# A conformer convolution: one channel tile's taps as products of token pairs, the last tile by token blocks, sums and second factor inside the norm's wait

## The chip, the cores and the metric

The kernel runs on one core of a Trainium2 chip. The metric is the device time of one execution in microseconds, given as the median of several runs; the time of before is 931.02 us (three runs, 930.98 to 931.54). Beside the runs there is one profiled execution, whose trace shows every engine: PE is TensorE (matrix products), PEld its weight loads, DVE VectorE, ACT ScalarE, POOL GpSimd, SP the engine that issues most DMAs.

## The reference

A trunk of two layers over 256 tokens of 1024 channels in float32. Each layer is half a SwiGLU FFN, a mixer, half a SwiGLU FFN, each behind an RMS norm and added to the residual stream; a final norm ends it. The mixer of the first layer is the convolution module, that of the second a latent attention. The change is in the convolution module:

```python
CONV_WIDTH = 31
def conv_module(h, w_pw1, w_dw, g_norm, w_pw2):
    u = h @ w_pw1                                  # 1024 -> 2048
    a, b = jnp.split(u, 2, axis=-1)
    u = a * jax.nn.sigmoid(b)
    u = lax.conv_general_dilated(                  # causal, depthwise: 31 taps per channel
        u, w_dw[:, None, :].astype(u.dtype), window_strides=(1,),
        padding=[(CONV_WIDTH - 1, 0)], dimension_numbers=("NWC", "WIO", "NWC"),
        feature_group_count=D_MODEL)
    u = jax.nn.silu(rmsnorm(u, g_norm))            # norm over the 1024 channels
    return u @ w_pw2                               # 1024 -> 1024
...
def reference(x, ...):
    h = x
    for i in range(DEPTH):
        h = h + 0.5 * swiglu_ffn(rmsnorm(h, ffn_norm1[i]), ...)
        m = rmsnorm(h, mix_norm[i])
        h = h + (conv_module(m, ...) if i % 2 == 0 else mla(m, ...))
        h = h + 0.5 * swiglu_ffn(rmsnorm(h, ffn_norm2[i]), ...)
    return rmsnorm(h, final_norm)
```

## The kernel before

**Weights.** All matrices come from memory as blocks of 128x2048 float32 (1 MB) through three raw buffers, in the order of the list `blocks`; a load is issued on SP and waits there until its raw buffer is free. Most blocks are split for TensorE into a high part (ScalarE copies to the reduced type float32r, L162) and a low part (VectorE subtracts, L163), in two pieces each, into five buffer pairs. A product of split factors is three products, low by high, high by high and high by low (`mm3`, and `mm` in the convolution with kinds "l", "h", "x"). The blocks of the convolution's first matrix (`cw1`, one for each of eight tiles of 128 channels) are used whole, from the raw buffer, without a split.

**Order.** The program is written in order and then scheduled; `order(a, b)` puts a behind b on an engine, functions marked `urgent` get priority, and `behind` puts a cast behind the last six urgent instructions of its engine. Each engine runs its own queue in the order that results, and waits at an instruction until its inputs are there.

**The convolution** (`conv_in`). Channels lie on partitions, tokens along the free dimension: eight tiles of 128 channels by 256 tokens. The tokens are two blocks of 128.

- *Projection* (`products`, L640). For each tile a gate and a factor u, each a sum over eight products of plain float32. Tiles 0 and 1 are done by token block, the others for 256 tokens at once, in the order of `CONV_STEPS` (0, 1, 2, 4, 3, 5, 6, 7). ScalarE makes the sigmoid of the gate (L649), VectorE multiplies (L650) into `V`, which has 30 zero columns ahead of the tokens.
- *Taps.* 31 taps for each tile. VectorE does tiles 0, 2, 4 and 5 and 17 taps of tile 7 (`taps_dve`, L684), one instruction a tap, accumulating in two PSUM banks. GpSimd does tiles 1 and 3 and 20 taps of tile 6 (`taps_pool`, L706): ScalarE writes the product of a tap into one of six buffers (L705), GpSimd adds it. TensorE does the remaining 11 taps of tile 6 and 14 of tile 7, for each token block (`taps_pe`, L716), as products with a 128x128 diagonal matrix, which ScalarE builds during the first FFN. Tiles 6 and 7 are the last ones (`CONV_LAST`) and are done by token block; an addition on VectorE (L818) joins their parts.
- *Norm.* ScalarE squares each tile (L728), TensorE sums over the channels by a product with ones of one column (`total`, L734). In `normed` ScalarE takes the mean (L749), GpSimd the power -1/2 (L751), ScalarE puts it on a diagonal (L753), TensorE spreads it over the partitions (`rb`, L761), VectorE scales (z, L768), ScalarE applies silu twice, once into the high part `Zh` (L772), and VectorE subtracts for the low part `Zl` (L774). This is done for each token block; `ends` starts it.
- *Second matrix* (`mm`, L849). For each token block eight steps f, in each of them six products of 512 columns. The first block's products run while the second block's taps are finished; the second block's sums stand behind step 4, its `rb` behind step 6, and the products of step 7 behind that.

The four blocks of the second matrix (`cw2`) are cast to high and low parts; three are loaded ahead of the blocks of `cw1`, the fourth behind them.

Of the kernel before, what the change touches and what calls it, by code (L numbers as in the profile page):

```python
# [29 lines left out]
PAD = TAPS - 1  # L30
H = 8
# [20 lines left out]
CONV_STEPS = ((0, 0), (1, 0), (0, 1), (1, 1), (2, None), (4, None), (3, None), (5, None), (6, None), (7, None))  # L52
CONV_TILES = (0, 1, 2, 4, 3, 5, 6, 7)
CONV_LAST = (7, 6)

CONV_ORDER = (0, 2, 1, 4, 5, 3, 7, 6)
# [23 lines left out]
def trunk(ctx: ExitStack, tc: tile.TileContext, x, xt, pos, invf, gains, gfin, wdw,  # L80
# [28 lines left out]
    for i in range(2):  # L109
        for w13, w2 in ((f1w13, f1w2), (f2w13, f2w2)):  # L110
# [33 lines left out]
    def load(src, pieces=1):  # L144
# [15 lines left out]
        for i in range(pieces):  # L160
            c = slice(i * n // pieces, (i + 1) * n // pieces)
            casts[len(loaded), i] = (nc.scalar.copy(hi[:, c], raw[:, c]),  # L162
                                     nc.vector.tensor_sub(lo[:, c], raw[:, c], hi[:, c].bitcast(F32)))  # L163
# [460 lines left out]
    def conv_in(act, X, make_next):  # L624
# [4 lines left out]
        Y = act.tile([P, KT, S], F32, tag="Y", name="Y")  # L629

        acc = [bank(t, "acc") for t in "CB"]
        for a in acc:
            behind(nc.vector.memset(a, 0.0))

        def products(i, part, t, u, after=None):

            w = loaded[conv_block[i]]
            for k in range(KT):
                c = slice(k * 2 * P + part * P, k * 2 * P + (part + 1) * P)
                mm = nc.tensor.matmul(u[:, t], w[:, c], X.x[:, k, t], start=(k == 0), stop=(k == KT - 1))  # L640
                if after is not None:
                    order(mm, after.ins)
            return mm

        @urgent
        def glu(i, t, gate, u):
            n = t.stop - t.start
            sg = tmp.tile([P, 512], F32, tag="s", name=uid("sg"))
            nc.scalar.activation(sg[:, :n], gate[:, t], AF.Sigmoid)  # L649
            nc.vector.tensor_mul(V[:, i, PAD + t.start:PAD + t.stop], u[:, t], sg[:, :n])  # L650

        every = slice(0, S)
        mm = None
        for n, (i, tb) in enumerate(CONV_STEPS):
# [8 lines left out]
            glu(i, t, gate, u)  # L663

        behind(nc.scalar.activation(small.tile([P, 1], F32, tag="silu", name="silu2"), neghalf, AF.Silu))

# [23 lines left out]
        def taps_pool(k, j0, j1, t):  # L690
# [3 lines left out]
            if k not in odd:  # L694
                odd[k] = act.tile([P, S], F32, tag="odd", name=uid("odd"))
            y = [(part[k] if k in part else Y[:, k, :])[:, t], odd[k][:, t]]
# [12 lines left out]
        def taps_pe(t, done):  # L709

            b = bank("A", "y")
            y = {}
            for i, (k, j0, j1) in enumerate(CONV_PE):
                y[k] = b[:, i * P:(i + 1) * P]
                for j in range(j0, j1):
                    mm = nc.tensor.matmul(y[k], diag[k][:, j - j0, :], V[:, k, j + t.start:j + t.stop],  # L716
                                          start=(j == j0), stop=(j == j1 - 1))
                    done.append(mm)
            return y

# [4 lines left out]
        def square(k, t):  # L725
            if k not in sq:
                sq[k] = act.tile([P, S], F32, tag="sq", name=uid("sq"), bufs=4)
# [18 lines left out]
        def normed(tb, after=()):  # L746
# [7 lines left out]
            if tb == 0:  # L754

                for ins in pool_last[-16:]:
                    order(ins, power.ins)
                order(prods_last[-6], ms_ins.ins)
                order(prods_last[-4], dgs[0].ins)
# [17 lines left out]
            if tb == 0:  # L777

                for ins in dve_last[-5:]:
                    order(ins, zs[1].ins)  # L780
                for ins in prods_last[-7:]:
                    order(ins, zhs[1].ins)

        for items, taps in ((CONV_DVE, taps_dve), (CONV_POOL, taps_pool)):
            for item in items:
                if item[0] in CONV_FIRST:
                    for tb in range(NT):
                        taps(*item, tbs(tb))
                elif item[0] not in CONV_LAST:
                    taps(*item, every)  # L790
# [4 lines left out]
        y, done = {}, {0: [], 1: []}  # L795
        sums = {}
        for tb in range(NT):
            t = tbs(tb)
            for item in CONV_DVE:
                if item[0] in CONV_LAST:  # L800
                    taps_dve(*item, t)
            for item in CONV_POOL:
                if item[0] in CONV_LAST:
                    taps_pool(*item, t)
            if tb == 0:
                for k in CONV_ORDER:
                    if k not in CONV_LAST:
                        for i in range(NT):
                            total(k, i)
            y[tb] = taps_pe(t, done[tb])  # L810
        def ends(tb, after, after_row):
# [4 lines left out]
            def add():  # L816
                for k in CONV_LAST:
                    last = nc.vector.tensor_add(Y[:, k, t], y[tb][k], part[k][:, t] if k in part else Y[:, k, t])  # L818
                    if tb == 1:

                        order(last, zs[3].ins)
                    sq_ins = square(k, t)
                    if tb == 0:

                        for ins in dve_last[3 - CONV_DVE[-1][2]:][:2]:
                            order(ins, last.ins)
                        order(prods_last[-10], sq_ins.ins)
                for k in CONV_LAST:
                    sums[tb] = total(k, tb)
# [435 lines left out]
```

## Time and profile before

| | before |
|---|---|
| median of three runs | 931.02 us |
| the profiled execution | 930.86 us |
| its span, first to last instruction | 929.1 us |
| TensorE busy | 918.9 us (99%) |
| VectorE, ScalarE, GpSimd busy | 584.7, 499.7, 90.0 us |
| mean granted TensorE clock | 0.997 |
| the convolution on TensorE, from the first projection to the next FFN's first product | 186.5 to 284.9 us |

Positions in the trace are microseconds from the span's start. A row of a timeline gives start, length, engine, line, operation, output and inputs, and the number of instructions merged into it; lengths of instructions that follow each other overlap, so the price of one in a row is the distance from start to start. What ended an idle time ahead of a row stands in brackets. A float32 product, which passes TensorE more than once, is two instructions in the trace. The granted clock is the share of full speed that TensorE's throttle allows.

### The profile page before, as it was taken

To read this page: it belongs to the slowest core of one execution; us is meant where nothing else is said; L and a number is where in the kernel's file an instruction comes from. 1 tells how busy PE (TensorE), PEld (TensorE's weight loads), DVE (VectorE), ACT (ScalarE), POOL (GpSimd) and SP (SyncE) were. 2 spreads that over 40 slices of the span, in tenths; PEclk is the share of its full clock that TensorE was granted. 3 is DMA by queue.
4 is the path that set the end of the run, shared out by engine and by line. 5 is a ranking of instruction groups with operands and counts; after the bars stand their busy time and mean duration, and the time that the engine had idled before them with its cause. 6 is when DMAs were issued, how large, how long until landed. Compare 5 with 4: busy or idle time off the path is not lost.

```text
span 929.1 us, 12053 instructions
## 1 busy us (share of the span) xinstructions
PE 918.9 (99%) x4374; PEld 772.2 (83%) x4374; DVE 584.7 (63%) x917; ACT 499.7 (54%) x852; POOL 90.0 (10%) x212
## 2 busy tenths in 40 slices
PE   9999999999999999999999999999999999999997
PEld 7888888898888888888888888888898888888886
DVE  5877664489977666664466666544666676656633
ACT  7964443477877554444374454434666574445421
POOL 1000000068932000000000000000200000000000
PEclk9999999999999999999999999999999999999999
DMA  9888775524315877676537777653451567677711
GB/s 341 309 305 278 248 241 209 182 92 158 116 46 219 285 238 254 229 248 224 181 141 266 246 252 245 237 206 121 178 185 46 188 231 246 241 236 244 245 46 46
DMA packets 60828, 191.55 MB, mean 206 GB/s; under 512 B 11232, under 2 KB 33376, under 8 KB 41440
## 3 DMA queue, kind: packets, MB, share of 16 engines
q1 hardware_dynamic: 60192, 190.09, 58.4%
q8 instruction: 34, 0.56, 0.2%
q10 hardware_dynamic: 576, 0.69, 0.2%
q14 instruction: 26, 0.21, 0.1%
HBM read 178.17 MB, written 12.58 MB: 205 GB/s over the span
## 4 chain that ended last, share of the span: by engine, by line
PE 94%; DVE 2%; ACT 1%; POOL 1%; issue 1%; DMA 0%; POOLq 0%; ACTq 0%; DVEq 0%
PE u L246 17%; PE u L249 17%; PE u L250 17%; PE o L246 9%; PE o L249 9%; PE o L250 9%; PE gate L640 3%; PE u L640 3%; PE o L849 2%; PE tp L290 1%; PE u L255 1%; DVE lo L163 1%; PE y L716 0%; PE sc L1089 0%; PE a L250 0%
## 5 line engine op out<-in xcount | busy, mean ns | idle before, releaser
L163 DVE TENSOR_TENSOR lo<-raw,hi 128x1024 fp32r<-128x1024 f32 x294 | 344.2, 1212 | 191.0 <-ACT hi L162 190.7
L162 ACT CAST hi<-raw 128x1024 fp32r<-128x1024 f32 x294 | 292.7, 1048 | 254.7 <-PE o L250 87.7
L246 PE MATMUL u<-lo,Xh 128*128 128x512 f32 x688 | 268.0, 390 | 0.5 <-ACT Xh L304 0.5
L249 PE MATMUL u<-hi,Xh 128*128 128x512 f32 x688 | 267.6, 389 | 0.0
L250 PE MATMUL u<-hi,Xl 128*128 128x512 f32 x688 | 267.2, 389 | 0.0
L246 PEld LDWEIGHTS u<-lo,Xh 128*128 128x128 f32 x688 | 129.1, 188 | 27.6 <-ACT Xh L304 0.7
L250 PEld LDWEIGHTS u<-hi,Xl 128*128 128x128 f32 x688 | 129.1, 188 | 26.8
L249 PEld LDWEIGHTS u<-hi,Xh 128*128 128x128 f32 x688 | 129.2, 188 | 26.6
L249 PE MATMUL o<-hi,Gh 128*128 128x512 f32 (+1 forms) x356 | 137.9, 387 | 0.0
L250 PE MATMUL o<-hi,Gl 128*128 128x512 f32 (+1 forms) x356 | 137.8, 387 | 0.0
L246 PE MATMUL o<-lo,Gh 128*128 128x512 f32 (+1 forms) x356 | 137.2, 387 | 0.0
L246 PEld LDWEIGHTS o<-lo,Gh 128*128 128x128 f32 x356 | 66.9, 188 | 13.5
L250 PEld LDWEIGHTS o<-hi,Gl 128*128 128x128 f32 x356 | 66.9, 188 | 13.5
L249 PEld LDWEIGHTS o<-hi,Gh 128*128 128x128 f32 x356 | 66.9, 188 | 13.4
L281 POOL TENSOR_TENSOR ms<-ss 128x1 f32<-128x1 f32 x16 | 8.0, 502 | 630.8 <-ACT junk L273 630.8
L564 DVE TENSOR_TENSOR Gl<-gb,Gh 128x512 fp32r<-128x512 f32 (+1 forms) x48 | 30.8, 645 | 45.2 <-ACT Gh L563 45.0
L563 ACT CAST Gh<-gb 128x512 fp32r<-128x512 f32 (+1 forms) x48 | 28.0, 584 | 55.6 <-DMA gb<-gd 55.5
L684 DVE SCALAR_TENSOR_TENSOR acc<-V,dw,acc 128x128 f32<-128x128 f32 (+1 forms) x168 | 56.0, 415 | 0.0
L705 ACT ACTIVATE prod<-V,dw 128x128 f32<-128x128 f32 (+1 forms) x123 | 46.6, 419 | 3.3 <-POOL Y L706 1.7
L611 DVE TENSOR_TENSOR s<-s,u 128x512 f32<-128x512 f32 (+1 forms) x48 | 30.5, 636 | 10.6 <-PE u L250 10.5
L610 ACT ACTIVATE s<-u,R 128x512 f32<-128x512 f32 (+1 forms) x48 | 31.2, 650 | 7.7 <-PE u L250 7.0
L553 DVE STREAM_TRANSPOSE gt<-s 128x512 f32<-128x512 f32 (+1 forms) x48 | 32.0, 667 | 1.4
(206 smaller groups left out, 836.6 us busy)
## 6 DMA issues: line engine op xcount, KB each, us to landing
raw<-in_f2w SPq DMA_DIRECT2D x66, 1024.0 KB, 4.9
raw<-in_f1w SPq DMA_DIRECT2D x62, 1024.0 KB, 5.1
raw<-in_cw SPq DMA_DIRECT2D x12, 1024.0 KB, 4.7
gd<-gt SPq DMA_DIRECT2D x160, 64.0 KB, 3.5
gb<-gd SPq DMA_DIRECT2D x40, 256.0 KB, 4.9
raw<-in_wo SPq DMA_DIRECT2D x4, 1024.0 KB, 4.9
raw<-in_wuq SPq DMA_DIRECT2D x3, 1024.0 KB, 4.7
raw<-in_f1w SPq DMA_DIRECT2D x8, 256.0 KB, 5.1
```

Of the source, the lines that this page charges most:

```text
L162: casts[len(loaded), i] = (nc.scalar.copy(hi[:, c], raw[:, c]), nc.vector.tensor_sub(lo[:, c], raw[:, c], hi[:, c].bitcast(F32)))
L163: nc.vector.tensor_sub(lo[:, c], raw[:, c], hi[:, c].bitcast(F32)))
L246: mm = nc.tensor.matmul(o, ah, bl, start=start, stop=False)
L249: nc.tensor.matmul(o, ah, bh, start=False, stop=False)
L250: return nc.tensor.matmul(o, al, bh, start=False, stop=stop)
L553: nc.vector.transpose(t[:, :w], g[:, :w].rearrange("p (t j q) -> p j t q", t=n, q=32))
L564: nc.vector.tensor_sub(Gl[:, f, tbs(tb)].rearrange("p t (i q) -> p t i q", q=32), bv, gh.bitcast(F32))
L610: nc.scalar.activation(s[:, :w], u[0, tb][:, :w], AF.Silu, scale=X.r[tb])
L611: nc.vector.tensor_mul(s[:, :w], s[:, :w], u[0, tb][:, w:] if both else u[1, tb])
L640: mm = nc.tensor.matmul(u[:, t], w[:, c], X.x[:, k, t], start=(k == 0), stop=(k == KT - 1))
L684: dve_last.append(nc.vector.scalar_tensor_tensor(out if j == j1 - 1 else y, v, w, y, op0=ALU.mult, op1=ALU.add))
L705: prods_last.append(nc.scalar.activation(p, v, AF.Copy, scale=w))
```

## The change

1. **Tile 6 on TensorE alone.** All taps of tile 6 become products of token pairs by 64 channels. A column of the moving operand holds 64 channels at an even and the same 64 channels at an odd token; the stationary operand `dpair` holds two tap weights for each pair of channel and token parity. 16 products of 128 columns make 128 pairs, so 256 tokens, of 64 channels; two groups of channels are 32 products (`pairs`). The GLU of tile 6 is written with the parities apart, ScalarE copies it in four 64-partition pieces into `VP` (the place of tile 6 in `V`), and four such copies bring the result from PSUM into `Y`. GpSimd builds `dpair` during the first FFN from a small input `wpair` (32 KB); ScalarE's 25 diagonals go.
2. **The last tiles are 5 and 7, by halves.** For the first block VectorE does 17 taps of tile 5 and all 31 of tile 7, for the second 14 and 17; GpSimd does the rest.
3. **Order.** Tile 3 is projected ahead of tile 4. Tile 7 is projected by token block; the second block's gate stands ahead of the pairs, its factor u behind the first block's sums, in the wait for the norm. Six of the second block's sums stand behind the first `rb`. In the second matrix the second block's last sums stand behind step 6 and its `rb` behind step 7 of the first block.
4. **Blocks.** The fourth block of `cw2` is loaded ahead of the blocks of `cw1`, and GpSimd makes its low part.
5. `Y` takes the place of an earlier tile, the clearing of VectorE's two PSUM banks goes, there are eight buffers of squares instead of four.

```diff
-CONV_DVE = ((0, 0, 31), (2, 0, 31), (4, 0, 31), (5, 0, 31), (7, 0, 17))
-CONV_POOL = ((1, 0, 31), (3, 0, 31), (6, 0, 20))
-CONV_PE = ((6, 20, 31), (7, 17, 31))
+CONV_DVE = (0, 2, 4)
+CONV_POOL = (1, 3)
...
+CONV_PAIRS = 6
+CONV_LAST = (5, 7)
+CONV_HALVES = {(5, 0): 17, (7, 0): 31, (5, 1): 14, (7, 1): 17}
+CONV_STEPS = ((0, 0), (1, 0), (0, 1), (1, 1), (2, None), (3, None), (4, None), (5, None), (6, None), (7, 0))
+CONV_TILES = (0, 1, 2, 3, 4, 5, 6, 7)
...
-                    for m in (-1, -2, -3, *CONV_TILES, -4):
+                    for m in (-1, -2, -3, -4, *CONV_TILES):
...
+            low = nc.gpsimd if len(loaded) == conv_block[-4] else nc.vector
             casts[len(loaded), i] = (nc.scalar.copy(hi[:, c], raw[:, c]),
-                                     nc.vector.tensor_sub(lo[:, c], raw[:, c], hi[:, c].bitcast(F32)))
+                                     low.tensor_sub(lo[:, c], raw[:, c], hi[:, c].bitcast(F32)))
...
+            apart = sg[:, n:].rearrange("p (s t) -> p t s", s=2)
+            pairs = [a.rearrange("p (t s) -> p t s", s=2) for a in (u[:, t], sg[:, :n])]
+            nc.vector.tensor_tensor(apart, *pairs, op=ALU.mult)
+            for g in range(2):
+                for q in range(2):
+                    nc.scalar.copy(VP[64 * q:64 * q + 64, g, PAD // 2:], apart[64 * g:64 * g + 64, :, q])
...
+        def pairs(after):
+            b = bank("A", "pairs")
+            for g in range(2):
+                for m in range(KP // 2):
+                    mm = nc.tensor.matmul(b[:, g * P:(g + 1) * P], dpair[:, g, 2 * m:2 * m + 2, :],
+                                          VP[:, g, m:m + P], start=(m == 0), stop=(m == KP // 2 - 1))
+                    order(mm, after.ins)
+                y = Y[64 * g:64 * g + 64, CONV_PAIRS, :].rearrange("p (t s) -> p s t", s=2)
+                for q in range(2):
+                    c = slice(64 * (1 - q), 64 * (1 - q) + 64)
+                    urgent(nc.scalar.copy)(y[:, q, :], b[c, g * P:(g + 1) * P])
+            return mm
+
+        last_gate, last_u = bank("A", "gate"), bank("A", "u")
+        mm = products(7, 1, tbs(1), last_gate, mm)
+        last_sg = sigmoid(last_gate, tbs(1))
...
+        mm = pairs(mm)
...
-        def taps_pe(t, done):
...
+        halves(0)
...
+        early = [k for k in CONV_ORDER if k not in CONV_LAST]
+        mm = sums_of(0, early, mm)
+        u_last = products(7, 0, tbs(1), last_u, mm)
+        glu(7, tbs(1), last_sg, last_u)
+        halves(1)
...
+        ends(0, mm)
+        for ins in last_products:
+            order(ins, sums[0].ins)
+        normed(0, (u_last,))
+        early_sums = sums_of(1, early, brow[0])
...
-                if tb == 0 and f == 4:
+                if tb == 0 and f == 0:
+                    for p in firsts:
+                        order(p, early_sums.ins)
+                elif tb == 0 and f == 6:
                     then = now[1]
-                elif tb == 0 and f == 5:
-                    behind_sums = list(firsts)
-                elif tb == 0 and f == 6:
-                    ends(1, then, now[0])
-                    for p in behind_sums:
+                elif tb == 0 and f == 7:
+                    ends(1, then)
+                    for p in firsts:
                         order(p, sums[1].ins)
-                    later[0, 7, 0] = later[0, 7, 1] = [brow[1]]
+                    normed(1, (now[1],))
...
+        ident2 = dpair[:, 1, KP - 1, :]
+        nc.gpsimd.tensor_tensor(ident2, ident[:, :64], ident[:, 64:], op=ALU.add)
...
+                    nc.gpsimd.tensor_tensor(dpair[:, g, j0:j1, :], ident2.unsqueeze(1).to_broadcast(full),
+                                            wp2[:, g, j0:j1].unsqueeze(2).to_broadcast(full), op=ALU.mult)
```

More of the change, by code (lines that the diff above doesn't have):

```diff
@@ L30 @@
 PAD = TAPS - 1
+KP = TAPS + 1
 H = 8
@@ L628, in conv_in @@
         nc.gpsimd.memset(V[:, :, :PAD], 0.0)
-        Y = act.tile([P, KT, S], F32, tag="Y", name="Y")
+        VP = V[:, CONV_PAIRS, :].rearrange("p (g t) -> p g t", g=2)
+        nc.gpsimd.memset(VP[:, 1, :PAD // 2], 0.0)
         acc = [bank(t, "acc") for t in "CB"]
-        for a in acc:
-            behind(nc.vector.memset(a, 0.0))
+        last_products = []
         def products(i, part, t, u, after=None):
             w = loaded[conv_block[i]]
+            last_products.clear()
             for k in range(KT):
@@ L707, in taps_pool @@
             pool_last.append(nc.gpsimd.tensor_tensor(y[0], y[0], y[1], op=ALU.add))
-        def taps_pe(t, done):
[L711 to L719, printed above, removed]
         msb = {}
@@ L793, in conv_in, with halves, sums_of, ends @@
                 square(k, every)
-        y, done = {}, {0: [], 1: []}
-        sums = {}
[L797 to L811, printed above, removed]
+        def halves(tb):
+            for k in CONV_LAST:
+                taps_dve(k, 0, CONV_HALVES[k, tb], tbs(tb))
+                if CONV_HALVES[k, tb] < TAPS:
+                    taps_pool(k, CONV_HALVES[k, tb], TAPS, tbs(tb))
+        def sums_of(tb, tiles, after):
+            for k in tiles:
+                mm = total(k, tb)
+                order(mm, after.ins)
+            return mm
+        sums = {}
+        def ends(tb, after):
             t = tbs(tb)
@@ L853, in mm @@
                     firsts.append(p)
-                    for a in later.pop((tb, f, d), ()):
-                        order(p, a.ins)
             return p
@@ L1158, in beside @@
     def beside():
-        for _ in range(4):
-            next(todo, None)
+        next(todo, None)
     X = Norm("ffn1_0", half=True)
```

102 lines of the change are left out of this document (57 added, 45 removed).

## The prediction

> **What bounds the kernel now.** I read the page's first part, then the timeline of TensorE through the convolution, then the clock by stretches, then the other engines' timelines around the places where TensorE waits.
>
> ```profile
> span 929.1 us, 12053 instructions
> PE 918.9 (99%) x4374; PEld 772.2 (83%) x4374; DVE 584.7 (63%) x917; ACT 499.7 (54%) x852; POOL 90.0 (10%) x212
> ```
>
> TensorE is busy for 99% of the span, so the time is TensorE's queue, and an edit is worth what it takes out of that queue or out of its waits. The change lies in the convolution. TensorE's timeline there (start, length, instructions; what ended an idle time stands in brackets; one fp32 product is two instructions):
>
> ```profile
> 199.88 1.95 PE L640 MATMUL u<-Xp,raw 128*128 128x128 f32 x16
> 201.67 3.62 PE L640 MATMUL gate<-Xp,raw 128*128 128x256 f32 x16
> ...
> 236.21 3.62 PE L640 MATMUL gate<-Xp,raw 128*128 128x256 f32 x16
> ...
> 243.11 1.84 PE L734 MATMUL ms<-ones,sq 128*128 128x1 f32 x16
> 244.81 7.84 PE L716 MATMUL y<-V,diag 128*128 128x128 f32 x68
> 252.49 0.95 PE L734 MATMUL ms<-ones,sq 128*128 128x1 f32 x8
> ...
> 255.08 0.38 PE L734 MATMUL ms<-ones,sq 128*128 128x1 f32 x2 [0.86 <-ACT sq L728]
> 256.24 0.38 PE L734 MATMUL ms<-ones,sq 128*128 128x1 f32 x2 [0.77 <-ACT sq L728]
> 256.48 2.97 PE L716 MATMUL y<-V,diag 128*128 128x128 f32 x18
> 259.24 0.63 PE L761 MATMUL rb<-dg,ones 128*128 128x128 f32 x2
> 259.67 1.81 PE L716 MATMUL y<-V,diag 128*128 128x128 f32 x8
> 261.24 0.48 PE L849 MATMUL o<-lo,Zh 128*128 128x512 f32 x1
> ...
> 268.20 0.50 PE L734 MATMUL ms<-ones,sq 128*128 128x1 f32 x4
> ...
> 271.41 0.38 PE L761 MATMUL rb<-dg,ones 128*128 128x128 f32 x2
> ...
> 273.02 0.39 PE L849 MATMUL o<-lo,Zh 128*128 128x512 f32 x1
> ```
>
> The reader is to see the prices. From start to start a 128-wide projection part takes 1.79 us (199.88 to 201.67), 68 tap instructions take 7.68 us (0.113 each), 16 instructions of the sums 1.70 us (0.106 each). Thirty products of 512 columns lie between 261.24 and 268.20: 0.232 each. TensorE stands still at 255.08 and 256.24, for the squares of the last tiles. And the 8 tap instructions at 259.67 take 1.57 us where 0.90 was due. The clock by stretches (the column before the DMA share is the granted clock) says why:
>
> ```profile
> 256.00:257.90 1.90, 1.66 (x14) 1.67 (x15) 1.90 (x9) 1.06 (x4) 0.91 (x2) 0.98 0.00 0
> 257.90:261.20 3.30, 3.30 (x18) 3.30 (x17) 1.49 (x6) 1.78 (x8) 2.95 (x8) 0.50 0.00 0
> 261.20:263.00 1.80, 1.80 (x10) 1.50 (x10) 1.80 (x9) 1.80 (x8) 1.36 (x3) 0.99 0.00 0
> ```
>
> After the two waits the clock is halved for 3.3 us, which costs half of that, 1.65 us. [...]
>
> **The change part by part.** Positions are those of the changed kernel's built instruction streams, prices those of the rows.
>
> *TensorE.* The 100 tap instructions (11.3 us) go. Tile 6 as token pairs is 32 products, 64 instructions of the same shape, 7.23 us: 4.1 us less. Tile 7's projections in halves are four parts of 1.79 us for two of 3.45 (201.67 row's pitch, 10 such parts to 236.21): 0.25 us more. The sums keep their count. I follow the new queue from 236.21, which nothing ahead of it moves if tile 2 is on time (below): three parts, 5.37 us, to 241.6; pairs to 248.8; five of the first block's sums to 249.9. Then the sums of tiles 6, 5 and 7 wait for the copies out of the pairs' bank and three squares on ScalarE. These are two 64-partition copies and a 256-wide and two 128-wide squares; by the 128-wide row below (0.28 at 192.12) some 0.25 each in a row, done at 250.3, last sum done at 250.65. About 0.5 us are waited. The second factor of tile 7 (u, 1.79) runs to 252.45.
>
> *The norm's chain* has these rows, of ScalarE and VectorE:
>
> ```profile
> 268.74 0.26 ACT L749 ACTIVATE msc<-ms,eps 128x1 f32<-128x1 f32 x1 [1.34 <-PE ms L734]
> 269.66 0.40 ACT L753 ACTIVATE dg<-ident,rc 128x128 f32<-128x128 f32 x1 [0.66 <-POOL rc L751]
> 271.83 1.13 DVE L768 SCALAR_TENSOR_TENSOR z<-Y,G,rb 128x128 f32<-128x128 f32 x4 [3.31 <-PE rb L761]
> 272.21 0.31 ACT L772 ACTIVATE Zh<-z 128x128 fp32r<-128x128 f32 x1 [2.15 <-DVE z L768]
> ```
>
> From the sums' end (268.70) to dg's end (270.06) are 1.36 us; from rb's start (271.41) to the first Zh's end (272.52) 1.11, some 1.4 with the weight load. In the first block the 1.79 us of u cover the 1.36 us. So rb starts at 252.45, the second block's six early sums (1.27 us) cover most of the 1.4 us, and the first product of o would start at 253.9. But ScalarE has the start of tile 7's second half ahead of Zh, which waits for u's GLU; Zh then ends at 254.3, and I take 254.6. That is 6.6 us before 261.24.
>
> In the second block the order turns against the change. Its sums now stand behind product 42 instead of 30: 254.6 + 42 x 0.232 = 264.3, sums 0.36, six products 1.39, rb at 266.1. But rb now stands behind the last product of the block, so nothing covers the 1.4 us to Zh: first product of the second block at 267.5. Before, it was 273.02. Gain 5.5 us. Behind it the streams are as before.
>
> *VectorE and GpSimd.* They must have the first block's taps ready by 250:
>
> ```profile
> 202.15 6.29 DVE L684 SCALAR_TENSOR_TENSOR acc<-V,dw,acc 128x128 f32<-128x128 f32 x24
> 222.31 0.48 DVE L682 TENSOR_SCALAR acc<-V,dw 128x256 f32<-128x256 f32 x1
> 235.21 0.42 DVE L686 TENSOR_TENSOR Y<-acc,Y 128x256 f32<-128x256 f32 x1
> 196.18 0.45 POOL L706 TENSOR_TENSOR Y<-Y,prod 128x128 f32<-128x128 f32 x1 [6.72 <-ACT prod L705]
> 220.67 0.45 POOL L707 TENSOR_TENSOR Y<-Y,odd 128x128 f32<-128x128 f32 x1
> 224.52 0.73 POOL L706 TENSOR_TENSOR Y<-Y,prod 128x256 f32<-128x256 f32 x1 [3.40 <-ACT prod L705]
> 241.68 0.72 POOL L706 TENSOR_TENSOR odd<-odd,prod 128x256 f32<-128x256 f32 x1
> 255.00 0.45 POOL L707 TENSOR_TENSOR part<-part,odd 128x128 f32<-128x128 f32 x1
> ```
>
> VectorE: a tap of 128 takes 0.26 us (6.29 for 24), tile 4 13.2 (222.31 to 235.55). Tile 4 now waits 0.6 us for its GLU and ends at 235.9. Then 48 taps of 128 (17 and 31, 12.5), two GLUs and two adds give 249.6. GpSimd: 60 adds from 196.18 to 221.1 (0.415 each), then tile 3, which no longer waits the 3.40 us because its projection is made one tile earlier: 30 adds of 0.686 (224.52 to 241.68 are 25), to 241.7, and 13 adds for tile 5 to 247.1. The same sum gives 253.0 for before, where the row says 255.45, so up to 2.4 us may be lost to ScalarE; even so it is in time: six product buffers, 2.5 us of adds, lie between ScalarE's stops (the sigmoid of tile 7's second gate, the table load behind it) and GpSimd. In the second block GpSimd's 23 adds behind the norm's power (251.7) end at 261.2 and VectorE's taps and z at 262.4, so its sums could run at 262.8, 1.5 us ahead of 264.3.
>
> *The moved block.* The last block of the second weight matrix is now loaded and cast ahead of the convolution, its low part on GpSimd:
>
> ```profile
> 192.12 0.28 ACT L649 ACTIVATE sg<-gate 128x128 f32<-128x128 f32 x1 [1.90 <-PE gate L640]
> 265.01 1.98 ACT L162 CAST hi<-raw 128x1024 fp32r<-128x1024 f32 x2
> 266.17 2.35 DVE L163 TENSOR_TENSOR lo<-raw,hi 128x1024 fp32r<-128x1024 f32 x2
> 278.87 4.62 DVE L163 TENSOR_TENSOR lo<-raw,hi 128x1024 fp32r<-128x1024 f32 x4
> 280.07 3.48 POOL L281 TENSOR_TENSOR ms<-ss 128x1 f32<-128x1 f32 x1 [10.44 <-ACT junk L273]
> DMA to landing us min/median/max: 4.6/4.7/5.9
> ```
>
> ScalarE's cast (1.98) falls into the 1.90 us it idled before 192.12, so it ends at 192.2. GpSimd's low part is not in the trace. Below stands VectorE's 2.35 us for both pieces, above 16 times the 128-wide add, 6.6; the line through 0.415 and 0.686 gives 2.3 a piece, 4.6, which I take as it is GpSimd's own row stretched: 191.2 to 195.8, just ahead of the first tap at 196.18. But tile 2's load now takes this block's raw buffer and so waits for it on SP, with tile 3's load queued behind: issued 195.9, landed (4.7) 200.6, wanted at 201.67. With 6.6 it is 0.9 us late.
>
> *Hidden.* The 32 pair weights on GpSimd (0.4 to 0.7 each by its add rows, under 20 us) replace 25 on ScalarE in the first FFN, where GpSimd is idle; their 32 KB load is one issue. The strided GLU of tile 6 (0.4 to 0.8) lies on VectorE with 0.3 us to spare.
>
> **The sum.** The profiled execution took 930.86 us, the median is 931.02: 931.0 - 5.5 = 925.5 us.
>
> **The rivals.** *The clock halves again.* [...] Before, 254.2 to 256.5 was thin and lost the clock, 243.11 to 244.81 was not enough. It would cost 1.65 again: 927.2.
>
> *The taps set the sums.* If GpSimd loses twice the 2.4 us, it is ready at 251.9 instead of 249.6, and the sums slip 2.2 us: 927.7. For it speaks that ScalarE feeds GpSimd in the same queue as squares and sigmoids; against it the 3.40 us saved.
>
> *Tile 2 comes late, and it is slower.* The row at 280.07 shows a 128x1 add of GpSimd that lasted 3.48 us, to the end of VectorE's four casts (278.87 to 283.49). [...] If each piece were held 3.3 us, tile 2 would be issued at 202.5 and, with the slowest landing, 5.9, come at 208.4: 6.7 us of waiting, 1.65 of halved clock, less 5.5: 933.9. It decides from 4.7 us of hold on (0.8 of slack, 5.5 of gain, less 1.65).
>
> **How the numbers follow.** Forecast 0.58 (925.5), clock 0.20 (927.2), taps 0.12 (927.7), tile 2 late 0.10, most of it slower. The forecast's bounds: without the waits at the sums and at Zh (0.5 and 0.7) 924.3, with tile 2 0.9 late 926.4. The range takes in both rivals that stay faster and something beyond them: 924.0 to 928.5. One measurement can tell 0.2%, 1.9 us. Faster by more 0.90, within 0.04, slower 0.06.
>
> **What would show it.** Right: 64 pair instructions at 0.113, o starting near 254.6 and the second block near 267.5, clock 1.00 from 245 to 265, a wait of over 1 us ahead of the second block only. Wrong: TensorE idle at 201.7 for the raw tile, a low part on GpSimd above 3 us a piece, clock rows of 0.50, or sums that wait for an add of VectorE that waits for GpSimd.

## The result, and the profile after

| | before | after |
|---|---|---|
| median | 931.02 us (7 runs, 929.86 to 932.49) | 928.28 us (7 runs, 927.18 to 929.22) |
| ratio | | 0.9967, 95% interval 0.9955 to 0.9978 |
| the profiled execution, its span | 930.86, 929.1 us | 928.28, 926.5 us |
| TensorE from the first projection to the next FFN's first product (below: the stage) | 98.40 us | 94.71 us |
| start of the first projection | 186.51 us | 187.67 us |

It is faster by 2.7 us, inside the range, and by half of the 5.5 us forecast. Within the profiled execution the stage is 3.69 us shorter, and the time behind it is the same to 0.1 us; but the stage starts 1.16 us later. What delays it is a load at the start. ScalarE waits for a DMA there, and the first split product comes at 17.98 us where it came at 16.94 before:

```profile
12.42 0.62 ACT L378 CAST hi<-raw 128x512 fp32r<-128x512 f32 x1 [1.96 <-DMA raw<-in_f1w]
17.98 0.50 PE L251 MATMUL u<-lo,Xh 128*128 128x512 f32 x1
```

In the second profile of the same kernel, below, it comes at 17.20, and in six of its eight variants at 17.06 to 17.39 (in the other two, whose products near 8 us take 1.06 us for two where the others take some 0.62, at 19.11 and 19.38). The change's own new load, of `wpair`, is issued later, at 22.5 us. That the late start is chance is likely, but not shown: three of the ten profiles of the changed kernel and its variants start late, none of the four of the kernel before and its variants. So I compare stages, and positions counted from each kernel's first projection.

The page's head and TensorE's timeline of after, in answer to the rows of before:

```profile
span 926.5 us, 12089 instructions
PE 915.1 (99%) x4370; PEld 767.8 (83%) x4370; DVE 585.6 (63%) x928; ACT 493.5 (53%) x841; POOL 118.8 (13%) x252
```

```profile
242.73 3.74 PE L692 MATMUL pairs<-V,dpair 128*128 128x128 f32 x32
247.50 3.81 PE L692 MATMUL pairs<-V,dpair 128*128 128x128 f32 x32 [1.03 <-ACT Y L179]
251.15 2.08 PE L764 MATMUL ms<-ones,sq 128*128 128x1 f32 x16
253.08 2.03 PE L648 MATMUL u<-Xp,raw 128*128 128x128 f32 x16
254.95 0.41 PE L792 MATMUL rb<-dg,ones 128*128 128x128 f32 x2
255.20 1.40 PE L764 MATMUL ms<-ones,sq 128*128 128x1 f32 x12
257.20 0.51 PE L890 MATMUL o<-lo,Zh 128*128 128x512 f32 x1 [0.60 <-ACT Zh L803]
...
267.17 0.50 PE L764 MATMUL ms<-ones,sq 128*128 128x1 f32 x4
...
269.08 0.49 PE L792 MATMUL rb<-dg,ones 128*128 128x128 f32 x2
270.35 0.51 PE L890 MATMUL o<-lo,Zh 128*128 128x512 f32 x1 [0.78 <-ACT Zh L803]
```

The queue is the one forecast, with one wait in it that was not: TensorE stands still for 1.03 us between the two groups of pairs, for ScalarE's copies (L179). What ScalarE does around it:

```profile
246.81 0.55 ACT L179 COPY Y<-pairs 64x128 f32<-64x128 f32 x2
...
251.35 0.55 ACT L179 COPY Y<-pairs 64x128 f32<-64x128 f32 x2 [1.36 <-PE pairs L692]
251.93 0.81 ACT L758 ACTIVATE sq<-Y 128x256 f32<-128x256 f32 x3
...
255.98 0.39 ACT L743 ACTIVATE part<-V,dw 128x128 f32<-128x128 f32 x1
256.27 0.39 ACT L743 ACTIVATE odd<-V,dw 128x128 f32<-128x128 f32 x1
...
256.85 0.30 ACT L803 ACTIVATE Zh<-z 128x128 fp32r<-128x128 f32 x1
```

The second group, which writes the other half of the bank, waited those 1.03 us until the copies out of the first group's half had ended. The squares then wait for the second group's copies at 251.35. Before the first Zh, ScalarE's queue has the start of tile 7's second half. The clock of this execution by stretches (the column before the DMA share):

```profile
252.00:256.00 4.00, 3.93 (x35) 3.84 (x36) 2.61 (x11) 3.30 (x12) 2.16 (x5) 1.00 0.00 0
256.00:260.00 4.00, 3.40 (x17) 2.60 (x17) 3.97 (x16) 4.00 (x16) 4.00 (x11) 1.00 0.77 264
260.00:264.00 4.00, 4.00 (x19) 3.16 (x19) 4.00 (x15) 3.01 (x11) 4.00 (x9) 1.00 0.00 0
```

None of these slices is halved. And GpSimd's low part, with which the block of the second matrix was paid for, took 2.34 us a piece, as forecast:

```profile
192.41 4.68 POOL L168 TENSOR_TENSOR lo<-raw,hi 128x1024 fp32r<-128x1024 f32 x2 [1.77 <-ACT hi L167]
```

My theory was then: a bank shared by the two groups costs about a microsecond, the uncovered row of the second block another, and the clock's half speed, seen before and not after, is luck as much as merit. The rivals were that the squares were late anyway, and that the clock follows from the waits alone.

### The profile page after: what moved, and what is told of

The parts are those of the page before. It is cut to its first block, busy times and chain, and to the rows that moved or that the text cites. A ratio compares the mean times of both kernels' runs of the same rounds, so it can differ in the third digit from the quotient of the medians.

```text
span 926.5 us, 12089 instructions
## 1 busy us (share of the span) xinstructions
PE 915.1 (99%) x4370; PEld 767.8 (83%) x4370; DVE 585.6 (63%) x928; ACT 493.5 (53%) x841; POOL 118.8 (13%) x252
## 4 chain that ended last, share of the span: by engine, by line
PE 93%; DVE 2%; ACT 2%; DMA 1%; issue 1%; POOL 0%; SPq 0%; POOLq 0%; ACTq 0%; DVEq 0%
PE u L251 17%; PE u L254 17%; PE u L255 17%; PE o L251 9%; PE o L254 9%; PE o L255 9%; PE gate L648 3%; PE u L648 3%; PE o L890 2%; PE tp L295 1%; DVE lo L168 1%; DMA raw<-in_f1w 1%; DMA xk<-in_xt 0%; PE sc L1128 0%; PE a L255 0%
## 5 line engine op out<-in xcount | busy, mean ns | idle before, releaser
L168 DVE TENSOR_TENSOR lo<-raw,hi 128x1024 fp32r<-128x1024 f32 (+1 forms) x292 | 343.6, 1217 | 185.0 <-ACT hi L167 184.7
```

The lines of the kernel that those rows point to most:

```text
L168: low.tensor_sub(lo[:, c], raw[:, c], hi[:, c].bitcast(F32)))
```

## The experiments

Each is the changed kernel with one to three edits, or the kernel before with one part of the change or with fillers. Times are medians; the kernel before stood at 931.4 to 931.5 beside them.

| kernel | median us | ratio to before, interval | stage us |
|---|---|---|---|
| banks apart | 926.55 | 0.9954, 0.9939 to 0.9969 | 93.33 |
| row one step earlier | 927.74 | 0.9963, 0.9948 to 0.9978 | 94.22 |
| Zh first | 927.35 | 0.9960, 0.9945 to 0.9974 | 94.66 |
| tile 7's factor early | 931.65 | 1.0001, 0.9992 to 1.0011 | 97.38 |
| tile 3 late again | 931.88 | 1.0002, 0.9987 to 1.0017 | 97.72 |
| tile 6 by diagonals | 931.52 | 1.0002, 0.9992 to 1.0011 | 98.84 |
| the changed kernel again | 928.75 | 0.9969, 0.9956 to 0.9982 | 96.06 |
| before, cast alone | 931.26 | 0.9998, 0.9987 to 1.0009 | 99.84 |
| before, seven fillers | 930.14 | 0.9989, 0.9979 to 0.9998 | 99.05 |
| before, fifteen fillers | 930.20 | 0.9988, 0.9979 to 0.9997 | 97.40 |
| banks and row | 926.31 | 0.9946, 0.9933 to 0.9958 | 93.37 |
| banks, row, one tap moved | 925.82 | 0.9941, 0.9927 to 0.9956 | 92.99 |

**Banks apart.**

```diff
-            b = bank("A", "pairs")
             for g in range(2):
+                b = bank("A", "pairs")
```

> The changed kernel, with each of the two groups of pairs in a bank of its own, so that the second group need not wait for ScalarE's copies out of the first group's bank (1.03 us idle ahead of it in the changed kernel's profile). Theory, the shared bank costs on the path: the idle ahead of the second group goes, the groups stand 3.7 to 3.9 us apart instead of 4.8, the second group's copies start near 250.3 instead of 251.35 (counted in that profile's time), the squares end near 251.75 instead of 252.74 because VectorE's parts are ready at 250.85 and 251.09, and the stage from the first projection to the second FFN's first product takes 93.7 to 93.9 us instead of 94.71; the median is 0.8 to 1.0 us lower, 927.3 to 927.5. Rival, VectorE's or ScalarE's work sets the squares: the groups move together but the stage stays at 94.5 to 94.8.

TensorE's, ScalarE's and VectorE's rows:

```profile
241.84 7.31 PE L692 MATMUL pairs<-V,dpair 128*128 128x128 f32 x64
...
250.53 0.83 PE L764 MATMUL ms<-ones,sq 128*128 128x1 f32 x6 [0.37 <-ACT sq L758]
...
254.94 0.50 PE L890 MATMUL o<-lo,Zh 128*128 128x512 f32 x1 [0.20 <-ACT Zh L803]
```

```profile
250.08 0.80 ACT L758 ACTIVATE sq<-Y 128x256 f32<-128x256 f32 x3
```

All 64 pair instructions run in one piece. Counted from the first projection, the squares end 0.97 us earlier, as expected (250.88 - 186.78 = 64.10, against 252.74 - 187.67 = 65.07), and the first product of o comes 1.37 us earlier (68.16 against 69.53). The 0.4 us beyond the expectation are won ahead of Zh, which TensorE now awaits for 0.20 us instead of 0.60; the row of VectorE's GLU for tile 7's last tokens shows what changed there. In the changed kernel it was released by the row `rb`, here by u (why one bank more does this is not shown):

```profile
255.57 0.29 DVE L664 TENSOR_TENSOR V<-u,sg 128x128 f32<-128x128 f32 x1 [1.39 <-PE rb L792]
```

```profile
253.36 0.29 DVE L664 TENSOR_TENSOR V<-u,sg 128x128 f32<-128x128 f32 x1 [0.33 <-PE u L648]
```

The whole 1.38 us arrives at the stage's end. The rival is out. In one bank the second group waited 1.03 us for copies out of other columns, in a bank of its own not at all; what holds it back in the shared one is not shown.

**The row one step earlier.** `ends` for the second block behind step 5 instead of 6, `rb` behind step 6 instead of 7, step 7 behind `rb`:

```diff
-                elif tb == 0 and f == 6:
+                elif tb == 0 and f == 5:
                     then = now[1]
-                elif tb == 0 and f == 7:
+                elif tb == 0 and f == 6:
                     ends(1, then)
...
+                elif tb == 0 and f == 7:
+                    for p in firsts:
+                        order(p, brow[1].ins)
```

> The changed kernel, with the second block's sums behind step 5 and its row rb behind step 6, so that step 7 (1.4 us of products) lies over the wait for the second block's first Zh. Theory: the 1.27 us between that rb and the next product goes; but the sums now come at 265.8 (in the changed kernel's time) where the last square is ready at 266.4, which costs 0.6, and step 6 (1.38 us) is a little shorter than the chain from the sums to the row (1.5), which costs 0.1 to 0.2: the stage takes 94.1 to 94.3 us instead of 94.71, the median 927.7 to 927.9. Rival, the wait only moves (the last tap of VectorE is late by more, or the chain behind the sums is longer without a step's cover): 94.7 to 95.2, no gain.

```profile
265.54 0.38 PE L764 MATMUL ms<-ones,sq 128*128 128x1 f32 x2 [0.37 <-ACT sq L758]
267.35 0.49 PE L792 MATMUL rb<-dg,ones 128*128 128x128 f32 x2
```

The wait behind `rb` is gone and one of 0.37 us for the last square has come; the stage is 0.49 us shorter, as expected.

**Zh first.** The two starts of tile 7's second half on ScalarE (`starts`, the instructions of L743) and two of its products go behind the first Zh.

```diff
+                for ins in starts[-2:] + prods_last[-12:-10]:
+                    order(ins, zhs[0].ins)
```

> The changed kernel, with the first four ScalarE instructions of tile 7's second-half part (about 1.1 us) put behind the first Zh of the first block, which stood ready behind them. Theory: the first Zh comes 0.3 to 0.5 us earlier, and with it the first output product (69.0 to 69.2 us behind the first projection instead of 69.53); GpSimd's taps of the last half come up to 0.5 us later but had 0.8 us of room at the end, where VectorE's last add is later; the second sums wait for VectorE, whose last taps don't move, so 0.2 to 0.4 us of the gain is given back there: the stage takes 94.3 to 94.7 us. Rival, nothing is given back: 94.2; other rival, GpSimd becomes last and the second sums are later: 94.8 to 95.3.

```profile
255.70 0.51 PE L892 MATMUL o<-lo,Zh 128*128 128x512 f32 x1 [0.18 <-ACT Zh L803]
...
266.06 0.50 PE L764 MATMUL ms<-ones,sq 128*128 128x1 f32 x4
```

The first product of o comes 0.43 us earlier (69.10 against 69.53), the second block's sums only 0.04 (79.46 against 79.50): the gain is given back ahead of those sums, as expected.

**Tile 7's factor early**, ahead of the pairs instead of in the norm's wait.

```diff
-        mm = pairs(mm)
+        u_last = products(7, 0, tbs(1), last_u, mm)
+        glu(7, tbs(1), last_sg, last_u)
+        mm = pairs(u_last)
...
-        normed(0, (u_last,))
+        normed(0, (sums[0],))
```

> The changed kernel, with the second factor of tile 7's last rows (16 products, 2.03 us) ahead of the pairs instead of in the wait for the norm's row. Theory, that wait is really filled by these products: the pairs, the copies and the squares come later by 1.8 us, the sums end by as much later, and behind them PE waits 1.5 to 1.7 us for the row with nothing to do, so the first output product comes 1.6 to 1.9 us later, 71.1 to 71.4 us behind the first projection instead of 69.53; VectorE gets the last rows of V some 10 us earlier and the second block isn't later for it; the stage takes 96.0 to 96.6 us instead of 94.71. Rival, the squares wait for VectorE anyway and the pairs had slack: the stage grows by less than 0.7 us. The clock may show a slice below 1.00 in the wait, which before it showed in no slice of this stage; that would add up to 1.6 us.

```profile
258.22 0.49 PE L794 MATMUL rb<-dg,ones 128*128 128x128 f32 x2 [1.66 <-ACT dg L785]
```

```profile
259.97:263.38 3.41, 3.41 (x9) 2.63 (x9) 3.41 (x14) 3.41 (x13) 3.41 (x8) 0.50 0.00 0
```

TensorE waits 1.66 us for the norm's row, and the first product of o is 1.35 us late, less than the 1.6 to 1.9 expected. A stretch at half clock does the rest: the second block's sums are 2.68 us late. The place in the norm's wait is worth 1.35 us, and what it spares the clock: the mean clock of this kernel's ten runs is 0.992 to 0.997.

**Tile 3 late again.**

```diff
-CONV_STEPS = (..., (2, None), (3, None), (4, None), ...)
-CONV_TILES = (0, 1, 2, 3, 4, 5, 6, 7)
+CONV_STEPS = (..., (2, None), (4, None), (3, None), ...)
+CONV_TILES = (0, 1, 2, 4, 3, 5, 6, 7)
```

> The changed kernel, with tile 4 ahead of tile 3 again, as before: the one part of the change that gives GpSimd tile 3 sooner is undone. Theory: GpSimd waits some 3 us for tile 3's first taps again, its part of tile 5's and 7's halves comes that much later (its part was ready at 248.25, and VectorE's at 250.56 takes it in), so the last add of tile 5 comes near 251.3 and the squares end 0.3 to 0.8 us later; the stage takes 94.9 to 95.6 us. Rival, the part has room enough and the stage stays within 0.2 us of 94.71; other rival, ScalarE's products for GpSimd pile up behind tile 3 and the sums are later by 2 us and more.

```profile
251.48 0.38 PE L764 MATMUL ms<-ones,sq 128*128 128x1 f32 x2 [0.36 <-ACT sq L758]
252.56 0.61 PE L764 MATMUL ms<-ones,sq 128*128 128x1 f32 x4 [0.69 <-ACT sq L758]
```

```profile
254.43:261.26 6.83, 6.83 (x27) 6.18 (x26) 5.99 (x23) 6.81 (x25) 6.83 (x16) 0.50 0.44 154
```

The products of u, which follow the sums, start 66.25 us behind the first projection instead of 65.41, so the squares are 0.84 us late, just above the expectation. The stage grows by 3.0 us, which I had not expected: 6.83 us at half clock follow. Six of the ten runs have a mean clock of 0.993 or less, below the 0.995 of the profiled one, so the median holds more half clock than this trace shows.

**Tile 6 by diagonals.** One product a tap in place of the 32 pair products, one copy out of the bank, the plain GLU.

```diff
-                    mm = nc.tensor.matmul(b[:, g * P:(g + 1) * P], dpair[:, g, 2 * m:2 * m + 2, :],
-                                          VP[:, g, m:m + P], start=(m == 0), stop=(m == KP // 2 - 1))
+                mm = nc.tensor.matmul(b[:, :S], diag[:, j, :], V[:, CONV_PAIRS, j:j + S],
+                                      start=(j == 0), stop=(j == TAPS - 1))
```

> The changed kernel, with all taps of tile 6 as products of plain 128x128 diagonals with 256 columns (31 products, 62 instructions of 0.226 us by twice the duration of one of 128 columns, 14.0 us in all) instead of the 32 products of token pairs (7.2 us and a wait of 1.03 us between their groups), and its V without the spreading copies. Theory, PE's own work ahead of the sums is what the pairs shorten: the sums come 5.5 to 6.0 us later and the stage takes 100.0 to 100.9 us, longer than before's 98.40. Rival, the taps of the other engines set the sums and the price of the products is partly hidden: less than 4 us longer.

```profile
241.71 13.55 PE L681 MATMUL pairs<-V,diag 128*128 128x256 f32 x62
```

Its sums start 4.96 us later than in the changed kernel, whose pairs with their wait take 8.4 us against 13.4. The stage is 4.13 us longer: 0.8 is won back at the second block, whose sums come 4.14 later. So the pairs are worth 4 us, less than the 5.3 us and more that I expected and just above the rival's bound. With them undone the median is that of before (931.52 us). But all ten of its runs have a mean clock of 0.998 or 0.999, and the runs of before with that clock take 930.1 (below): at the same clock it is 1.4 us slower than before.

**The changed kernel again.**

> The changed kernel once more, unaltered. Its first profile had no slice of the convolution below a clock of 1.00, and its first split product at 17.98 us, where the kernel before had 16.94 and four of its own variants 17.06 to 17.24. Theory: the late load at the start was an accident, the first split product comes at 17.0 to 17.3, the stage takes 94.6 to 94.8 us with the clock at 1.00, and the profiled execution 927.1 to 927.5 us. Rival, the clock's window falls into this stage in some executions: 96.2 to 96.5 us for the stage with a window of 3.41 us at 0.50. Other rival, the start is late again (17.8 and more) and is this kernel's own.

```profile
253.54:256.95 3.41, 2.81 (x23) 2.63 (x23) 2.27 (x9) 3.37 (x12) 3.41 (x9) 1.00 0.51 142
256.95:260.36 3.41, 3.41 (x10) 2.52 (x9) 3.41 (x14) 3.41 (x13) 3.41 (x8) 0.50 0.40 168
260.36:264.00 3.64, 3.64 (x17) 2.97 (x17) 3.64 (x13) 1.71 (x7) 3.54 (x8) 1.00 0.01 2
```

The start was not late (17.20), and up to the first product of o the stage is the same as in the first profile to 0.01 us (69.53). Then the clock is halved for 3.41 us: the stage takes 96.06, 1.35 us more. The same kernel has both clocks.

**Before, with the cast alone.**

```diff
-                    for m in (-1, -2, -3, *CONV_TILES, -4):
+                    for m in (-1, -2, -3, -4, *CONV_TILES):
...
+            low = nc.gpsimd if len(loaded) == conv_block[-4] else nc.vector
...
-                                     nc.vector.tensor_sub(lo[:, c], raw[:, c], hi[:, c].bitcast(F32)))
+                                     low.tensor_sub(lo[:, c], raw[:, c], hi[:, c].bitcast(F32)))
```

> The kernel before, with one part of the change alone: the fourth second-matrix block is loaded ahead of the convolution's tiles and the low part of its cast is GpSimd's (two instructions of 128x1024, 4.6 to 4.7 us in all, ahead of GpSimd's first tap). Theory, it is hidden: GpSimd's first tap comes near 197 us instead of near 193 and its parts are still ready ahead of the squares, tile 2's products come on time, the stage stays within 0.4 us of 98.40. Rival, GpSimd's taps set the sums and everything behind the sums moves by up to 4 us: 100 to 102; other rival, VectorE had been slowed by that cast and the stage gets shorter by 0.5 to 1.

```profile
191.66 4.68 POOL L164 TENSOR_TENSOR lo<-raw,hi 128x1024 fp32r<-128x1024 f32 x2 [1.77 <-ACT hi L163]
```

```profile
256.65 0.59 PE L735 MATMUL ms<-ones,sq 128*128 128x1 f32 x2 [0.78 <-ACT sq L729]
```

```profile
256.23:263.06 6.83, 6.41 (x30) 6.41 (x31) 3.60 (x15) 3.00 (x11) 3.86 (x9) 0.50 0.00 0
```

The last sum starts 69.74 us behind the first projection, in before 69.73: the cast is hidden to the hundredth. Yet the stage is 1.44 us longer, since the clock stays halved for 6.83 us here and 3.41 there.

**Before, with fillers in the two waits for the squares**, first seven products of zeros, then fifteen (eight and seven), into unused columns of the taps' bank.

```diff
+                    if t.start and len(done) == 11:
+                        for _ in range(7):
+                            f = nc.tensor.matmul(b[:, 2 * P:], still[:, :P], still, start=True, stop=True)
+                            order(f, (fill or done)[-1].ins)
+                            fill.append(f)
```

> The kernel before, with seven idle bf16 products of 128x256 (0.22 us each) put into the two waits for the squares (four ahead of the first of the last two sums, three ahead of the second), and one tap of the second block moved behind them. Nothing else is changed. Theory, the clock halves because PE had 2.2 us of almost no work there: with the products in the waits the granted clock stays at 1.00 through 258 to 261 us, the stage gets shorter by 1.3 to 1.7 us less up to 0.3 that the fillers may delay the sums: 96.9 to 97.4 us instead of 98.40, the median 929.5. Rival, the halving comes from something else (the taps' own work before it, or it is due at that time anyway): the clock still falls to 0.50 for 3.3 us and the stage takes 98.3 to 98.7.

```profile
253.00:256.41 3.41, 2.31 (x19) 1.70 (x19) 2.58 (x11) 2.50 (x8) 2.35 (x6) 1.00 0.01 2
256.41:259.82 3.41, 3.41 (x17) 3.41 (x18) 1.75 (x7) 1.58 (x5) 2.66 (x7) 0.50 0.00 0
```

A filler took 0.12 us, not the 0.22 I had taken, so 0.67 and 0.43 us of wait were left, and this execution still lost the clock. Eight of its ten runs have a mean clock of 0.998 or more all the same, and the median is 1.35 us lower than that of before beside it.

> The kernel before with 15 idle bf16 products instead of seven in the two waits for the squares: they took 0.12 us each, not 0.22, so seven left 0.67 and 0.43 us of wait; eight fill the first wait of 0.86 and seven the second of 0.77 but for 0.1. Theory, the waits and thin sums cause the clock's window at half: without them no slice of 252 to 264 us is below 1.00, and the stage takes 96.7 to 97.1 us instead of 98.40. Rival, idle products of zeros do not count for the throttle, or something else sets it: one window of 3.41 us at 0.50 stays (98.4 to 99.1), or two (100 to 100.8).

```profile
253.97 1.04 PE L723 MATMUL y<-still 128*128 128x256 bf16 x8
255.22 0.38 PE L741 MATMUL ms<-ones,sq 128*128 128x1 f32 x2 [0.21 <-ACT sq L735]
255.47 0.92 PE L723 MATMUL y<-still 128*128 128x256 bf16 x7
```

```profile
254.00:256.00 2.00, 1.79 (x17) 1.39 (x15) 1.23 (x6) 1.15 (x4) 1.44 (x4) 1.00 0.01 4
256.00:258.00 2.00, 2.00 (x18) 1.72 (x16) 2.00 (x9) 1.14 (x4) 0.86 (x2) 1.00 0.00 0
```

Nothing is halved, and the mean clock of every run is 0.998 or 0.999, where the kernel before has values from 0.995. In this kernel the waits do cost the clock. The stage is 1.0 us shorter, at 97.40 a little behind the expectation: the first product of o is 1.27 us earlier, and 0.27 is lost again further on.

**Banks and row together**, the two edits above.

> The changed kernel with both of the edits that shortened its stage: a bank of its own for each group of pairs (93.33 us alone), and the second block's row one step earlier (94.22 us alone). Theory, they are independent, since the first ends ahead of the first output product and the second begins behind it: 94.71 - 1.38 - 0.49 = 92.84 us for the stage, in bounds 92.6 to 93.2, and a median of 925.8 to 926.4. Rival, the second block's squares then are later against the products by what the first block gained (VectorE's taps of the second half don't move with the sums), so the wait for them grows from 0.37 us to 1 us and more: 93.3 to 93.8. The granted clock is expected to stay at 1.00; a window at half, 3.41 us long, would cost 1.7.

```profile
264.89 0.38 PE L764 MATMUL ms<-ones,sq 128*128 128x1 f32 x2 [0.94 <-ACT sq L758]
```

The two edits don't add: the wait for the last square grows to 0.94 us and the stage stays at 93.37, as the rival said.

**One tap moved**, in the same kernel, with the places in the lists of instructions shifted by one:

```diff
-CONV_HALVES = {(5, 0): 17, (7, 0): 31, (5, 1): 14, (7, 1): 17}
+CONV_HALVES = {(5, 0): 17, (7, 0): 31, (5, 1): 14, (7, 1): 16}
```

> The kernel of banks and row together (stage 93.37 us, where PE waited 0.94 us for the last square at the second block's sums) with one tap of tile 7's second half given from VectorE (0.28 us) to GpSimd (0.43 us), whose part was ready 1.1 us ahead of VectorE's in that kernel. Theory, VectorE's last taps set those sums: the wait falls to 0.6 to 0.7 and the stage to 93.0 to 93.15 us. Rival, GpSimd's or ScalarE's longer part takes the place of it, or the scheduler's order of VectorE's work moves the end: 93.3 to 93.6. A window of the clock at half would add 1.3 to 1.7.

```profile
266.24 0.38 PE L764 MATMUL ms<-ones,sq 128*128 128x1 f32 x2 [0.59 <-ACT sq L758]
```

VectorE's taps set those sums: a tap less, and the wait falls to 0.59 and the stage to 92.99. At 925.82 us this version is the fastest of all; its interval overlaps that of banks apart, and by the stage it is 0.34 us ahead of it.

## Why the prediction was half right

**Right in mechanism, and nearly in size, up to one wait.** The queue, the 0.113 us of a pair instruction (3.74 us for 32), the norm's chain under u and the uncovered row of the second block (1.27 us, forecast 1.4) all came. Counted from the first projection:

| | before | forecast shift | after | banks apart |
|---|---|---|---|---|
| first product of o | 74.73 | -6.6 | 69.53 (-5.20) | 68.16 (-6.57) |
| first product of the second block | 86.51 | -5.5 | 82.68 (-3.83) | 81.31 (-5.20) |
| end of the stage | 98.40 | -5.5 | 94.71 (-3.69) | 93.33 (-5.07) |

**The step that failed** is "pairs to 248.8": I laid 64 instructions end to end, though both groups write one bank and ScalarE copies out of it between them. I had even counted those copies, but behind the pairs only. The wait and what hangs on it are 1.38 us by the experiment; without it the first product of o stands within 0.1 us of the forecast. That it comes so near is in part luck: with the banks apart u starts 0.3 us later than forecast (64.44 us against 250.65 - 186.51 = 64.14), and TensorE waits 0.20 us for Zh where I had put 0.7. The remaining 0.43 us of the stage lie behind that point: 13.15 us from the first block's to the second block's first product instead of 12.9, most of it in the 42 products, which take 9.97 us instead of 9.74, and 0.14 more behind it.

**The second failure is that the clock was taken as one state.** The forecast counted the whole 1.65 us of half clock in before as gained, and gave its return a chance of 0.20. In fact before has it in most executions but not in all, and the changed kernel in about half. The lists of runs show it by each run's mean clock: in the profiled executions 0.998 or more goes with no halved stretch in the stage, 0.996 or 0.997 with one of 3.41 us, and 0.995 with one of 6.83 us. Of 72 runs of the kernel before beside these kernels, 13 have a clock of 0.998 or more and a median of 930.1 us, 46 have 0.996 or 0.997 and 931.5, and 13 have 0.995 and 932.6. Of twelve runs of the changed kernel, six have 0.998 or more (927.9, among them the one whose profile shows the late start) and six 0.996 or 0.997 (928.8). At the same clock the change gives 2.2 to 2.7 us.

**The account closes by stages.** Of the 5.5 us, 1.38 went to the shared bank and 0.43 to what lies behind the first product of o; that leaves the 3.69 us between the two profiled stages. Of these, 1.00 is the clock that before lost, since fifteen fillers take its stage from 98.40 to 97.40 us; the forecast had priced it at 1.65. At a whole clock on both sides 2.69 us are left (97.40 to 94.71). In the profiled pair the clock took nothing away from the forecast, since the changed kernel had it whole there; that pair lost 1.16 us by the late start instead, and six of the other eleven runs lost by the clock.

**The clock rival** had its price nearly right (1.35 us measured, 1.65 named) and its chance wrong. Its 0.20 was my estimate; six of twelve runs of the changed kernel have the lower clock. What lies ahead of a halved stretch differs. At the end of the program TensorE's last product of before ends at 922.8 us, and the clock is halved from 926.84, after 4.0 us without a product. In the stage TensorE was busy for 2.81 of the 3.41 us ahead of the halved stretch in the changed kernel's second profile, 1.40 of them with sums of one column.

How one program can have both clocks is not shown. In the changed kernel's first profile the same place, 254.47 to 257.88 us, holds the same 2.81 us of TensorE's work, 1.40 of them sums of one column, and the clock stays at 1.00 there and in the 3.41 us behind it.

**The taps** were in time: VectorE's add with GpSimd's part ran at 250.56, ahead of the squares, which waited for the pairs. Tile 3 ahead of tile 4 is worth 0.8 us at the squares.

```profile
250.56 0.33 DVE L849 TENSOR_TENSOR Y<-part,Y 128x128 f32<-128x128 f32 x1
```

**Tile 2** was not late, and the cast on GpSimd cost nothing in either kernel: 4.68 us against 4.6, with no sign of the hold that the slower rival needed (3.3 us a piece). That rival's slack of 0.8 us is 1.1 by the prediction's own positions (201.67 - 200.6), which changes nothing here.

What is open: what halves the clock. In the 3.41 to 3.47 us ahead of the six halved stretches TensorE was busy for 1.81 to 2.81 us; but the changed kernel's first profile has 2.81 us in such a stretch too and kept the clock. Open too is what the other parts of the change are worth, which were not undone one by one (the halves of tiles 5 and 7, the early gate and the six early sums); and how many of the runs at 928.3 to 928.6 with a whole clock started late, since only one of them has a profile.

## What to carry to other kernels

Where two groups of products share a PSUM bank and another engine empties the first, price the second group from the end of that copy, or give it a bank of its own: here the shared bank cost 1.03 us of wait and 1.38 us of the stage. Where a profile shows a stretch at half clock, do not book its end as the gain of an edit: here one kernel had it in some executions and not in others (six of twelve runs of the changed kernel have a mean clock of 0.996 or 0.997, six 0.998 or more). Look at the mean clock of every run, and compare runs at the same clock. An edit that shortens the first half of a stage pays only as far as the second half's inputs move with it; ask what sets those, here VectorE's taps.

## What the runs showed of the hardware

The granted clock was 0.50 for a stretch of the stage in six of the traces here: for 3.41 us in before (257.83 to 261.24), in the changed kernel's second profile (256.95 to 260.36), with tile 7's factor early (259.97 to 263.38) and with seven fillers (256.41 to 259.82), and for 6.83 us in before with the cast alone (256.23 to 263.06) and with tile 3 late (254.43 to 261.26). TensorE had waited in the stage no longer than 1.66 us at once ahead of it. The changed kernel, with the same waits in both (1.03 and 0.60 us), had it in one profiled execution and not in the other. With fifteen products of zeros in two waits of 0.86 and 0.77 us the mean clock was 0.998 or 0.999 in each of ten runs. A filler of 128x256 in bf16 took 0.12 us, half of what I had read for it at the program's start (4.39 us for 20). The profile's clock row says 1.00 in both places; why the first ones took twice as long is not shown.
